# DeltaNet's values and outputs turned by VectorE and placed by the write to DRAM

## The chip, the cores and the metric

The kernel runs on one core of a Trainium2 chip. The metric is the device time of one execution in microseconds (us). Before the change it is 1200.37 us, the median of three runs (1199.62 to 1200.76).

## What is computed

One layer of a hybrid decoder over 1024 tokens of width 1024, in float32. One input projection feeds two mixers: a gated DeltaNet (4 heads of 128, computed in chunks) and a dilated sliding-window attention (8 heads of 64). Their outputs are concatenated, projected and added to the input; a gated MLP with a depthwise convolution follows, and a last norm. The change touches the DeltaNet mixer's values and outputs. The reference, cut to them:

```python
def gated_delta_rule(q, k, v, g, beta):
    ...
    rhs = jnp.concatenate([vc, gam * kc], axis=-1)
    sol = lax.linalg.triangular_solve(lmat, rhs, left_side=True, lower=True, unit_diagonal=True)
    u_v, w_k = sol[..., :Dv], sol[..., Dv:]
    ...
    def step(state, xs):
        uv, wk, qd, at, ke, ge = xs
        u = uv - jnp.einsum('bhck,bhkv->bhcv', wk, state)
        o = jnp.einsum('bhck,bhkv->bhcv', qd, state) + jnp.einsum('bhcj,bhjv->bhcv', at, u)
        state = ge[..., None, None] * state + jnp.einsum('bhck,bhcv->bhkv', ke, u)
        return state, o
    ...

def hybrid_layer(x, ...):
    h = rmsnorm(x, norm1_w)
    proj = h @ w_in
    ...
    qkv_a = jax.nn.silu(causal_dwconv(qkv_a, conv_qkv_w)).astype(jnp.float32)
    ...
    o_a = gated_delta_rule(qa, ka, va, g, beta)
    z = z_a.astype(jnp.float32).reshape(B, S, GDN_HEADS, GDN_HEAD_DIM)
    o_a = (rmsnorm(o_a, gdn_norm_w) * jax.nn.silu(z)).reshape(B, S, GDN_WIDTH).astype(x.dtype)
    ...
    x = x + jnp.concatenate([o_a, o_b], axis=-1) @ w_out
```

## The kernel before

**Layouts.** The projection leaves each of its columns (128 features) as a tile of 128 features by 1024 tokens, features on partitions. The DeltaNet chain wants values with tokens on partitions: a tile `vtok` of 128 tokens by 8 chunks by 128 features. Its outputs come out in that layout too, and the output projection wants features on partitions again. So values and outputs must be turned, 128x128 by 128x128, 8 such blocks a head each.

**Order on TensorE.** The `Weave` class plans one fixed order of TensorE's instructions. Each piece of work is a generator with a level; a generator yields how long it wants to wait by the planner's own costs, and the planner takes the ready one of the lowest level. A `slack` is added to a wait, so it says how long after an operand's planned time the consumer is placed. The projection (`dense`) is the filler of the highest level: 25 columns in the order of the list `DENSE` (line 42), each 48 matmuls of 128x512 (two halves, 8 rows of k, three products of high and low parts), written by `mm3`. The other engines' orders come from the scheduler, which follows what the tiles wait for; operations through `uv` and `ua` are given high priority. Nearly all DMAs are issued by SyncE (SP), in order. Because the operations run through helpers, most rows of the profile carry a helper's line: L139 and L141 for other engines and DMAs, L192 for matmuls, L196 for 128x128 transposes.

**The work around the change**, in the order in which the chip meets it:

- `dense` (507) evicts each half column from PSUM with VectorE into `xr` (or `aqkv` for attention's columns). For a query, key or value column `conv_silu` adds the causal convolution (three VectorE steps) and the silu (ScalarE), giving `qT`, `kT` or `vT`.
- `kprep` (586) and `qprep` (640) transpose keys and queries on TensorE for their norms, and make the chunk matrices; `qprep` parks query and matrix in DRAM (`qpark`, `atpark`).
- `vprep` (666) calls `tokens` (567): two batches of four TensorE transposes of `vT` into PSUM, then eight ScalarE activations that scale by the key's norm `nk` on the way into `vtok`.
- `forward_sub` (672) inverts the 32x32 blocks of all heads on VectorE (31 steps on `xi`) and stores `xi` and its turned copy `mt` to `xdram` and `xtdram`. `merges` (700) loads them (`x`, `um`) and builds the 128x128 inverses on TensorE; its first products are the group `x,um`.
- `chain` (798) runs the 8 chunks of one head, four heads interleaved, each step in turn on TensorE, VectorE and ScalarE. Its result goes back into `vtok`.
- `finish` (867) transposes a head's outputs on TensorE (two batches of four), ScalarE copies each PSUM bank to `ot` times the norm weight `gw2`, and SP stores it to `mixer`.
- The last four projection columns are the gates (`z`). Each loads its head's outputs (`og` from `mixer`); `gate` (483) multiplies them by silu of the column, and `mixer_splits` (1081) splits the gated head into high and low parts `ohi` and `olo` for `out_proj`.
- `attention` (902) waits for the chains of heads 0 and 1, then for the outputs of all heads (`("o", h)`), then for its first columns, and loads its operands with `att_load` (884). Each of its four groups takes a pair of heads.

Of the kernel before, what the change touches and what calls it, by code (L numbers as in the profile page):

```python
# [38 lines left out]
TSLACK = -1.0, -0.6  # L39
URGENT = 400  # L40
MGAP = 0.6
DENSE = ([("k", 3), ("a", 0, 0), ("a", 0, 1)] + [(c, h) for h in range(4) for c in "qv"] + [("a", 0, 2)]
         + [("a", p, i) for p in (1, 2, 3) for i in range(3)] + [("z", h) for h in range(4)])

# [100 lines left out]
def hybrid_layer(tc, I, out):  # L145
# [25 lines left out]
    def A(name, tag, dt=F32, shape=(P, 1024)):  # L171
        if tag in TURNS:
            i = turns[tag] = turns.get(tag, -1) + 1
            tag = TURNS[tag][i % len(TURNS[tag])]
        return tile_(lp, shape, dt, name, tag, SLOTS[tag])
# [72 lines left out]
    apark = dp.tile([4, 2, P, S], F32, name="apark")  # L248
    avdram = dp.tile([4, 32, 32, P], F32, name="avdram")
    qpark = dp.tile([H, P, S], F32, name="qpark")  # L250
    atpark = dp.tile([H, P, S], F32, name="atpark")
    xpark = dp.tile([KT, P, S], F32, name="xpark")
    upark = dp.tile([FT, P, S], F32, name="upark")
# [4 lines left out]
    def next_bank(tag, *tiles, slack=0.0):  # L258

        while max(wv.need(*tiles), wv.slot_free(tag, 2)) + slack > 1e-3:  # L260
            yield max(wv.need(*tiles), wv.slot_free(tag, 2)) + slack
        return bank(tag)

    def half(i):
        return slice(i * 512, i * 512 + 512)
# [180 lines left out]
    def scaled(pair, name, by_class=False, tag="ev", t=None, hs=(0, 1)):  # L446
        if t is None:
            t = A(name, tag)
        for h in hs:
            sl = half(h)  # L450
            if by_class:
                ve.tensor_tensor(t[:, sl].rearrange("p (n c u) -> p n u c", n=4, c=4),
                                        pair[h].rearrange("p (n u c) -> p n u c", n=4, c=4),
                                        rstdB[:, sl].rearrange("p (n u c) -> p n u c", n=4, c=4), op=OP.mult)
            else:
                ve.tensor_tensor(t[:, sl], pair[h], rstdB[:, sl], op=OP.mult)
        return t
# [22 lines left out]

    put_off = []

    def gate(og, xr, anchor=None):
        y = A("zz", "ev")
        insts = [ac.activation(y, xr, AF.Tanh, scale=0.5),
                 ve.scalar_tensor_tensor(y, y, 1.0, xr, op0=OP.add, op1=OP.mult),
                 ve.tensor_tensor(og, og, y, op=OP.mult)]
        last["og"] = insts[2:]
        if anchor is not None:
            after(insts[0], anchor[0], "the softmax goes first")  # L490
            after(insts[1], anchor[1], "the softmax goes first")
# [15 lines left out]
    def dense():  # L507

        yield from wv.until("first")
        yield from wv.until("norms")  # L510
        wv.add(2, first_keys())

        raw = [raw_weight(I["wi"][0])]
        nxt = wk(None, raw.pop())
        raw.append(raw_weight(I["wi"][1]))
        for i, col in enumerate(DENSE):
            kind, h = col[:2]
            if kind == "z":
                yield from wv.until(("o", h))
            w = nxt  # L520
            if i + 1 < len(DENSE):
                nxt = wk(None, raw.pop())
            if i + 2 < len(DENSE):
                raw.append(raw_weight(I["wi"][i + 2]))
            pair = []
            for hh in range(2):
                pt = bank("hf")
                yield wv.need(pt, *w)
                for k in range(KT):
                    mm3(pt, [t[:, k, :] for t in w], [t[:, half(hh)] for t in xs[k]], k == 0, k == KT - 1)  # L530
                    yield 0.0

                pair.append(pt)
                if hh == 0:
                    while put_off:
                        gate(*put_off.pop(0))
                    xr = A("aqkv" if kind == "a" else "xr", "go" if kind == "k" else "ev")
                scaled(pair, "xr", kind == "a", t=xr, hs=(hh,))
            if kind == "k":
                T["k", h] = conv_silu(xr, 4 + h, "kT", "kT*")  # L540
                wv.add(3, kprep(h))
            elif kind == "q":
                q = conv_silu(xr, h, "qT", "qa")
                wv.add(4, qprep(h, q))
            elif kind == "v":
                v = conv_silu(xr, 8 + h, "vT", "qa")
                wv.add(4, vprep(h, v))
            elif kind == "z":
                og = gated[h] = A("og", "kT*")
                sy.dma_start(og, mixer[h])  # L550
                if i + 1 < len(DENSE):
                    put_off.append((og, xr))
                else:
                    gate(og, xr)
            else:
                if col[2] < 2:
                    sy.dma_start(apark[h, col[2]], xr)
                else:
                    t = A("avt", "ev")
                    ve.transpose(t.rearrange("p (c n j) -> p n c j", c=4, n=NCH), by_block(xr))  # L560
                    for b in range(4):
                        sq_.dma_start(avdram[h].rearrange("u x (b j) -> b u x j", b=4)[b],
                                     t[32 * b:32 * b + 32].rearrange("u (x j) -> u x j", j=32))
                wv.done.add(col)
        wv.done.add("dense")

    def tokens(src, dst, scale=None, ss=None):

        for hh in range(2):
            pt = yield from next_bank("atr", src)  # L570
            for c in range(4):
                i = 4 * hh + c
                tp(pt[:, c * P:(c + 1) * P], src[:, i * P:(i + 1) * P])
            if dst is not None and scale is None:
                ua.activation(dst[:, half(hh)], pt, AF.Copy)
            for c in range(4):
                i = 4 * hh + c
                if scale is not None:
                    ua.activation(dst[:, i * P:(i + 1) * P], pt[:, c * P:(c + 1) * P], AF.Copy,
                                         scale=scale[:, i:i + 1])  # L580
                if ss is not None:
                    sq = tile_(sp, [P, P], F32, "sq", ("osq", "w2", "w3")[i % 3], 1)
                    ua.activation(sq, pt[:, c * P:(c + 1) * P], AF.Square, accum_out=ss[:, i:i + 1])
        return dst
# [80 lines left out]

    def vprep(h, vT):
        yield from wv.until(("q", h))
        yield wv.need(vT, slack=SLACK)
        G[h]["vtok"] = yield from tokens(vT, A("vtok", ("dv", "dw")[h % 2]), G[h]["nk"])
        wv.done.add(("v", h))  # L670

    def forward_sub():
# [192 lines left out]
        wv.add(1, finish(h, vtok))  # L865

    def finish(h, osb):
        for hh in range(2):
            pt = yield from next_bank("atr", osb, slack=0.8)
            for c in range(4):  # L870
                i = 4 * hh + c
                tp(pt[:, c * P:(c + 1) * P], osb[:, i * P:(i + 1) * P])
            ot = tile_(sp, [P, 512], F32, "ot", "t2", 2)
            ac.activation(ot, pt, AF.Copy, scale=gw2)
            sy.dma_start(mixer[h][:, half(hh)], ot)
        wv.done.add(("o", h))


# [23 lines left out]
    def attention():  # L902
# [1 line left out]
            yield from wv.until(("c", h, NCH - 1))  # L904
        mk = A("mk", "go", shape=(P, 448))
        sy.dma_start(mk, I["mk"])
        for h in range(H):
            yield from wv.until(("o", h))
        yield from wv.until(("a", 0, 2))
        cur = att_load(0)  # L910

        def scores(pair):

# [167 lines left out]
    def mixer_splits():  # L1081
        yield from wv.until("dense")
        load_residual(MORDER[0])
        load_residual(MORDER[1])
        wv.done.add("residual")
        for i in range(8):
            yield from wv.until(("o", i))
            ots[i] = (X("ohi"), X("olo"))
            if i < H:
                lo = split(gated[i], *ots[i])  # L1090
                last.setdefault("olo", []).append(lo)
                if i and "probabilities" in last:
                    after(lo, last["probabilities"], "the probabilities go first")
            else:
                src = A("ot", "ev")
                for h in range(2):
                    sl = half(h)
                    if i < 7 or h == 0:
                        sy.dma_start(src[:, sl], mixer[i][:, sl])
                    split(src[:, sl] if i < 7 or h == 0 else last["oT"], *[t[:, sl] for t in ots[i]])  # L1100
            yield wv.need(*ots[i])
            wv.done.add(("ot", i))
# [656 lines left out]
```

## Time and profile before

| | us |
|---|---|
| median of three runs | 1200.37 |
| the profiled execution | 1200.24 |
| its span | 1198.5 |
| stage from the projection's key columns to the merges' loads | 97 to 184 |
| merges | 184 to 225 |
| chain | 225 to 292 |
| from the chain's end to attention's first scores | 292 to 311 |
| attention, with the rest of the projection | 311 to 470 |

The page gives busy time per engine over the whole span. A row of a group reads: line, engine, operation, outputs and inputs by the program's names, shape, count, then busy us and mean ns of one, then the engine's idle time just before. A row of the timeline reads: start, busy time, engine, line, operation, names, shape and count of what runs in a row; a bracket at its end is the idle time before it and what ended that. Starts are in us from the span's start.

### The profile page before, as it was taken

What the parts mean: (1) busy time and instruction counts of PE and PEld (TensorE: products, weight loads), DVE (VectorE), ACT (ScalarE), POOL (GpSimd) and SP (SyncE); (2) the same over time, 40 slices, a digit from 0 to 9 for tenths busy, and PEclk for the clock granted to TensorE, in tenths of its full rate; (3) what the DMA queues carried; (4) which work ended last, traced back from release to release, by engine and by line L of the source; (5) the groups of instructions that cost most, each with busy time, mean ns of one, the idle gap of its engine ahead of it and who ended that gap; (6) DMA issues with size and microseconds to landing.
All of it is one profiled execution on the core that took longest, in us unless ns stands there. A gap on an engine that the chain in (4) does not pass through costs nothing.

```text
span 1198.5 us, 18275 instructions
## 1 busy us (share of the span) xinstructions
PE 1187.8 (99%) x7026; PEld 983.1 (82%) x7026; DVE 962.0 (80%) x1536; ACT 571.4 (48%) x1121; POOL 55.1 (5%) x50
## 2 busy tenths in 40 slices
PE   9999999999999999999999999999999999999997
PEld 7888888898777777888888888888888888888887
DVE  7686985584677687777898888989888889898987
ACT  7383344363444344555454544445454453445452
POOL 0212110013000000000000000000000000000001
PEclk9999999999999999999999999999999999999999
DMA  7323234537543314343222223131222395356734
GB/s 237 106 75 103 75 121 131 150 114 216 163 118 104 98 37 146 144 158 106 74 71 102 85 74 106 53 106 58 101 89 70 104 378 212 118 182 218 238 100 156
DMA packets 97448, 152.72 MB, mean 127 GB/s; under 512 B 37808, under 2 KB 48848, under 8 KB 97360
## 3 DMA queue, kind: packets, MB, share of 16 engines
q1 hardware_dynamic: 96640, 151.02, 38.5%
q8 instruction: 55, 0.90, 0.3%
q10 hardware_dynamic: 720, 0.53, 0.1%
q14 instruction: 33, 0.27, 0.1%
HBM read 115.59 MB, written 35.93 MB: 126 GB/s over the span
## 4 chain that ended last, share of the span: by engine, by line
PE 96%; DVE 2%; ACT 1%; issue 1%; DMA 0%; POOL 0%; DVEq 0%; ACTq 0%; POOLq 0%
PE ps L192 46%; PE pa L192 20%; PE dw L192 17%; PE pc L192 10%; PE ps L196 1%; PE ps L201 1%; DMA wst<-in_wu 0%; DVE sm L141 0%; PE warm L192 0%; DVE x1h L139 0%; ACT sm L141 0%; DVE aqkv L139 0%; DVE T L139 0%; DVE wst L139 0%; DVE pair L139 0%
## 5 line engine op out<-in xcount | busy, mean ns | idle before, releaser
L192 PE MATMUL dw<-pr 128*128 128x512 f32 (+1 forms) x984 | 211.4, 376 | 0.0
L192 PEld LDWEIGHTS dw<-pr 128*128 128x128 f32 x984 | 176.7, 188 | 33.7
L192 PE MATMUL ps<-xhi,whi 128*128 128x512 f32 x448 | 184.5, 412 | 0.0
L192 PE MATMUL ps<-xhi,wlo 128*128 128x512 f32 x448 | 175.2, 391 | 0.0
L192 PE MATMUL ps<-xlo,whi 128*128 128x512 f32 x448 | 174.8, 390 | 0.0
L192 PE MATMUL pa<-T,pair 128*128 128x512 f32 x528 | 127.1, 390 | 0.3 <-ACT u L139 0.2
L192 PEld LDWEIGHTS pa<-T,pair 128*128 128x128 f32 x528 | 98.9, 188 | 21.3 <-ACT u L139 0.8
L192 PEld LDWEIGHTS ps<-xhi,whi 128*128 128x128 f32 x448 | 84.4, 188 | 19.5 <-issue 3.6
L192 PEld LDWEIGHTS ps<-xhi,wlo 128*128 128x128 f32 x448 | 84.1, 188 | 18.5
L192 PEld LDWEIGHTS ps<-xlo,whi 128*128 128x128 f32 x448 | 84.5, 189 | 14.3
L139 ACT ACTIVATE u<-pa 128x512 f32<-128x512 f32 x44 | 26.3, 599 | 109.7 <-PE pa L192 109.6
L139 DVE SCALAR_TENSOR_TENSOR y<-xu,fcw,y 128x1023 f32<-128x1023 f32 (+1 forms) x44 | 56.3, 1280 | 24.4 <-ACT y L139 24.4
L139 ACT ACTIVATE pr<-wd 128x1024 fp32r<-128x1024 f32 x33 | 35.0, 1061 | 76.1 <-DVE wd L139 36.9
L139 ACT ACTIVATE whi<-wst 128x1024 fp32r<-128x1024 f32 (+2 forms) x38 | 38.5, 1013 | 62.9 <-PE ps L192 52.7
L192 PE MATMUL pa<-B,A 128*128 128x512 f32 x264 | 63.5, 389 | 0.0
L192 PE MATMUL pa<-T,S 128*128 128x512 f32 x264 | 63.4, 389 | 0.0
L192 PE MATMUL pc<-B,pair 128*128 128x512 f32 x264 | 63.4, 389 | 0.0
L192 PE MATMUL pc<-T,S 128*128 128x512 f32 x264 | 63.4, 389 | 0.0
L139 DVE TENSOR_TENSOR wst<-wst 128x512 f32<-128x512 f32 x88 | 60.3, 686 | 0.8
L192 PE MATMUL ps<-B,pair 128*128 128x512 f32 x252 | 60.5, 389 | 0.0
L141 ACT ACTIVATE sm<-sm,mx 128x128 f32<-128x128 f32 (+7 forms) x64 | 35.5, 556 | 50.1 <-DVE mx L141 50.1
L192 PEld LDWEIGHTS pc<-B,pair 128*128 128x128 f32 x264 | 49.5, 188 | 10.3
(244 smaller groups left out, 2241.4 us busy)
## 6 DMA issues: line engine op xcount, KB each, us to landing
wst<-in_wu SPq DMA_DIRECT2D x44, 512.0 KB, 3.7
wd<-in_wd SPq DMA_DIRECT2D x44, 512.0 KB, 4.4
wst<-in_wi SPq DMA_DIRECT2D x25, 512.0 KB, 3.7
upark<-y SPq DMA_DIRECT2D x22, 512.0 KB, 3.6
r<-upark SPq DMA_DIRECT2D x22, 512.0 KB, 9.5
wa<-in_wd SPq DMA_DIRECT2D x22, 256.0 KB, 3.0
apark<-aqkv SPq DMA_DIRECT2D x8, 512.0 KB, 2.7
wst<-in_wo SPq DMA_DIRECT2D x8, 512.0 KB, 3.7
```

The costliest lines, as they stand in the source:

```text
L139: return getattr(eng, op)(*a, **kw)
L141: return getattr(eng, op)(*a, **kw)
L192: tc.stamp_issue_order_token(nc.tensor.matmul(dst, lhs, rhs, start=start, stop=stop, **kw).ins, TOKEN)
L196: tc.stamp_issue_order_token(nc.tensor.transpose(dst, src, ident).ins, TOKEN)
L201: tc.stamp_issue_order_token(nc.tensor.transpose(dst, src[rows], ident[rows, rows]).ins, TOKEN)
```

## The change

Values: `vprep` turns `vT` in place with one VectorE transpose, which turns each 32x32 block by itself; four stores to a new DRAM tile `vdram` put the blocks where they belong, one load brings back `vtok`, and eight activations scale it in SBUF. Outputs: `finish` turns 32x32 blocks with four VectorE transposes of 128x256 (tile `ft`, with a pause of 0.4 us of planned time after each) and stores once; the blocks are left in a permuted order in `mixer`. The gate columns are therefore written permuted on eviction, `og` is loaded by four DMAs with runs of 1 KB, and the gated heads are put back in token order by the split. The factor `gw2` moves into `gate`. Attention no longer waits for the outputs of all heads; it loads first and then waits for the chains of heads 2 and 3.

In number: 64 TensorE transposes and 8 `ot` copies go; 4 VectorE transposes of 128x1024 and 16 of 128x256 come, and SP issues 16 stores to `vdram`, 4 loads of `vtok`, 12 more loads of `og` and 4 fewer stores to `mixer`.

In the built order of TensorE, the projection matmuls ahead of the first merge product are as many as before; one `qT,kT` group of four has moved behind it, and each transposing batch of a query is 6 projection matmuls later. Between the last chain product and attention's first scores stand 6 projection matmuls (before: 72 and 8 transposes); 18 more stand inside the chain, and a block of 78 (before: 3 and 36) ahead of attention's third group. On VectorE the inversion's last steps and the copy of `mt` have moved behind the eviction of the last query's second half. On SP each load of `vtok` stands behind its four stores and waits for them.

```diff
+FSLACK = 0.5
...
+    vdram = dp.tile([H, P, S], F32, name="vdram")
...
+    def by_row(t):
+        return t.rearrange("p (a c i) -> p a c i", a=4, c=NCH)
+
+    def by_token(t):
+        return t.rearrange("p (c a i) -> p a c i", a=4, i=32)
+
     def gate(og, xr, anchor=None):
         y = A("zz", "ev")
         insts = [ac.activation(y, xr, AF.Tanh, scale=0.5),
                  ve.scalar_tensor_tensor(y, y, 1.0, xr, op0=OP.add, op1=OP.mult),
-                 ve.tensor_tensor(og, og, y, op=OP.mult)]
+                 ve.scalar_tensor_tensor(og, og, gw2, y, op0=OP.mult, op1=OP.mult)]
...
-                scaled(pair, "xr", kind == "a", t=xr, hs=(hh,))
+                if kind == "z":
+                    ve.tensor_tensor(by_row(xr)[:, :, 4 * hh:4 * hh + 4], by_token(pt), by_token(rstdB[:, half(hh)]), op=OP.mult)
+                else:
+                    scaled(pair, "xr", kind == "a", t=xr, hs=(hh,))
...
                 og = gated[h] = A("og", "kT*")
-                sy.dma_start(og, mixer[h])
+                for b in range(4):
+                    sq_.dma_start(og[32 * b:32 * b + 32].rearrange("j (a y) -> j a y", a=4),
+                                 mixer[h].rearrange("(a j) (b y) -> b j a y", a=4, b=4)[b])
...
     def vprep(h, vT):
         yield from wv.until(("q", h))
-        yield wv.need(vT, slack=SLACK)
-        G[h]["vtok"] = yield from tokens(vT, A("vtok", ("dv", "dw")[h % 2]), G[h]["nk"])
+        yield wv.need(vT, slack=1.0)
+        vtok, nk = A("vtok", ("dv", "dw")[h % 2]), G[h]["nk"]
+        ve.transpose(vT, vT)
+        blocks = vdram[h].rearrange("(a t) (c b i) -> b t c a i", a=4, c=NCH, b=4)
+        for b in range(4):
+            sq_.dma_start(blocks[b], vT[32 * b:32 * b + 32].rearrange("t (c a i) -> t c a i", c=NCH, a=4))
+        sy.dma_start(vtok, vdram[h])
+        yield wv.need(vtok)
+        for c in range(NCH):
+            cs = slice(c * P, (c + 1) * P)
+            ua.activation(vtok[:, cs], vtok[:, cs], AF.Copy, scale=nk[:, c:c + 1])
+        G[h]["vtok"] = vtok
         wv.done.add(("v", h))
...
     def finish(h, osb):
-        for hh in range(2):
-            pt = yield from next_bank("atr", osb, slack=0.8)
-            for c in range(4):
-                i = 4 * hh + c
-                tp(pt[:, c * P:(c + 1) * P], osb[:, i * P:(i + 1) * P])
-            ot = tile_(sp, [P, 512], F32, "ot", "t2", 2)
-            ac.activation(ot, pt, AF.Copy, scale=gw2)
-            sy.dma_start(mixer[h][:, half(hh)], ot)
+        yield wv.need(osb, slack=FSLACK)
+        t = A("ft", "kT*")
+        by_feature, src = t.rearrange("p (b c i) -> p b c i", b=4, c=NCH), osb.rearrange("p (c b j) -> p b c j", c=NCH, b=4)
+        for b in range(4):
+            ve.transpose(by_feature[:, b], src[:, b])
+            yield 0.4
+        sy.dma_start(mixer[h], t)
         wv.done.add(("o", h))
...
-        for h in range(H):
-            yield from wv.until(("o", h))
         yield from wv.until(("a", 0, 2))
         cur = att_load(0)
+        for h in range(2, H):
+            yield from wv.until(("c", h, NCH - 1))
...
-                lo = split(gated[i], *ots[i])
+                g4, hi4, lo4 = by_row(gated[i]), by_token(ots[i][0]), by_token(ots[i][1])
+                ac.activation(hi4, g4, AF.Copy)
+                lo = ve.tensor_tensor(lo4, g4, hi4.bitcast(F32), op=OP.subtract)
```

## The prediction

> **What bounds the kernel now.** I read the page's head and the engine shares of the chain that ended last.
>
> ```profile
> span 1198.5 us, 18275 instructions
> PE 1187.8 (99%) x7026; PEld 983.1 (82%) x7026; DVE 962.0 (80%) x1536; ACT 571.4 (48%) x1121; POOL 55.1 (5%) x50
> PE 96%; DVE 2%; ACT 1%; issue 1%; DMA 0%; POOL 0%; DVEq 0%; ACTq 0%; POOLq 0%
> ```
>
> TensorE (PE) is busy 99% of the span and carries 96% of the chain, so a matmul that is taken away is worth its time unless it stood in a wait. The view by windows shows that for the stages the change touches: projection with the first preparation, merges, chain, the stage between, attention. Columns are the window, its length, then each engine's busy us with its instructions, granted clock, DMA share, GB/s.
>
> ```profile
> core 0: us, PE busy (x) PEld busy (x) DVE busy (x) ACT busy (x) POOL busy (x), PEclk, DMA share, GB/s
> 97.00:184.00 87.00, 87.00 (x449) 73.91 (x448) 73.31 (x153) 34.84 (x94) 13.59 (x8) 1.00 0.31 99
> 184.00:225.00 41.00, 41.00 (x590) 35.28 (x589) 20.47 (x31) 14.84 (x41) 2.96 (x3) 1.00 0.55 153
> 225.00:292.00 67.00, 65.94 (x447) 59.86 (x446) 43.44 (x125) 37.26 (x137) 13.13 (x10) 1.00 0.45 149
> 292.00:311.00 19.00, 19.00 (x102) 15.11 (x101) 7.85 (x22) 5.52 (x14) 3.54 (x2) 1.00 0.79 198
> 311.00:470.00 159.00, 158.27 (x1699) 121.17 (x1698) 119.77 (x320) 66.69 (x201) 3.65 (x8) 1.00 0.32 99
> ```
>
> PE shows idle time of 1.06 us in the chain and 0.73 in attention, none elsewhere; the clock is full throughout. VectorE is the second engine: 84% busy in the first window, 65% in the chain.
>
> **What goes from PE.** 64 transposes, in two groups of the view by instruction.
>
> ```profile
> L196 PE MATMUL ps<-ident,vtok 128*128 128x128 f32 x32 | 4.6, 273 | 0.0
> L196 PE MATMUL ps<-ident,vT 128*128 128x128 f32 x32 | 4.2, 274 | 0.0
> ```
>
> The 273 ns of one overlap with the next, so I price a batch by the starts around it in the timeline (start, busy, engine, group).
>
> ```profile
> 127.36 0.40 PE L192 MATMUL ps<-xhi,wlo 128*128 128x512 f32 x1
> 127.60 1.04 PE L196 MATMUL ps<-ident,vT 128*128 128x128 f32 x8
> 128.39 0.47 PE L192 MATMUL ps<-xhi,whi 128*128 128x512 f32 x1
> 128.70 0.39 PE L192 MATMUL ps<-xlo,whi 128*128 128x512 f32 x1
> 128.93 0.40 PE L192 MATMUL ps<-xhi,wlo 128*128 128x512 f32 x1
> ...
> 271.37 0.60 PE L196 MATMUL ps<-ident,vtok 128*128 128x128 f32 x4
> 271.73 0.48 PE L192 MATMUL ps<-xhi,whi 128*128 128x512 f32 x1
> 272.05 0.39 PE L192 MATMUL ps<-xlo,whi 128*128 128x512 f32 x1
> ```
>
> Projection matmuls follow each other at about 0.227 us. Without the batch two of them, in the place of 128.39 and 128.70, would start at 127.60 and 127.83; the second came at 128.70, so eight transposes cost 0.88 us (0.09 of it the first matmul after them, 0.31 to its follower instead of 0.23). The group of four costs 272.05 − 271.37 − 0.227 = 0.45. The vT transposes stand as four eights: 3.5 us. Of the vtok ones six fours (2.7) and one eight (0.9): 3.6. **Sum −7.1.** The projection, the merges and attention keep their matmuls.
>
> **The value's new way.** Per head VectorE turns vT, SP issues four stores to DRAM (runs of 128 bytes) and one load that waits for them, and ScalarE scales eight tiles, now from SBUF.
>
> ```profile
> L139 DVE STREAM_TRANSPOSE avt<-aqkv 128x1024 f32<-128x1024 f32 x4 | 5.0, 1245 | 0.1
> L139 SPq DMA_DIRECT2D avdram<-avt x16: 584/664/2220, 212.8 to 397.8; - x16
> DMA to landing us min/median/max: 2.7/3.5/4.3
> qT<-apark SPq DMA_DIRECT2D x4, 512.0 KB, 3.8
> 179.68 2.16 ACT L141 ACTIVATE vtok<-ps,nk 128x128 f32<-128x128 f32 x8
> 183.92 1.06 ACT L139 ACTIVATE qT<-qT 128x1024 f32<-128x1024 f32 x1 [2.08 <-DVE qT L139]
> 189.51 1.03 PE L196 MATMUL ps<-ident,qT 128*128 128x128 f32 x8
> 225.82 0.94 PE L192 MATMUL ps<-vtok,um 128*128 128x128 f32 x7
> ```
>
> The second and third rows are the existing turned values' store (issue ns and landing, min/median/max), the nearest to the new one; the fourth is a load of the same size. So 1.25 + 3×0.66 + 3.5 + 3.8 + 2.16 ≈ 12.7 us from silu to scaled. Its cover is the time until PE's first product with vtok at 225.82: head 3's stores stand in SP's queue behind the merge loads (issued until about 196, below), so its values are ready at about 210, 15 us early. If that cover were gone, the 12.7 would stand open once. The nearer danger is what queues behind: SP sits about 3.5 us in the load's wait for each head, and ScalarE's eight scalings stand ahead of the next head's query silu. For head 2 the scalings end near 184.8, the silu near 185.9; PE wants that query at 189.51, pulled ahead by three vT batches (2.64) and pushed back 1.36 by six projection matmuls that the built order puts ahead of it: 188.2, so 2.3 us of room. Heads 0 and 1 have about 1.5. I cost it at nothing; at the bad ends (landing 4.3, 0.8 over; issue and load 1.1 over) heads 0 and 1 lose 0.4 each.
>
> **The merges.** In VectorE's built order the inversion's last steps and the copy of mt have moved behind the eviction of the last query's second half, and its convolution stands between them.
>
> ```profile
> 174.02 0.32 SPq L139 DMA_DIRECT2D xdram<-xi  x1
> 175.15 0.32 SPq L139 DMA_DIRECT2D xtdram<-mt  x1
> 177.90 0.69 DVE L139 TENSOR_TENSOR xr<-ps,rstdB 128x512 f32<-128x512 f32 x1 [2.78 <-PE ps L192]
> 178.76 1.23 DVE L139 TENSOR_TENSOR wlo<-wst,whi 128x1024 fp32r<-128x1024 f32 x1 [0.17 <-ACT whi L139]
> 179.91 3.92 DVE L139 SCALAR_TENSOR_TENSOR qT<-xr,gcw,qT 128x1023 f32<-128x1023 f32 x3
> 178.36 1.91 SPq L139 DMA_DIRECT2D x<-xdram  x4
> L139 SPq DMA_DIRECT2D um<-xtdram x16: 432/449/487, 180.4 to 189.9; - x16
> DMA to landing us min/median/max: 1.8/1.9/3.6
> 198.42 2.21 PE L192 MATMUL ps<-x,um 32*32 32x32 f32 x128
> ```
>
> After: xr cannot start before 177.90 − 2×0.88 = 176.1; its 0.69, wlo's 1.23 and one of the three convolution steps (3.92 / 3 = 1.3) make 179.4, and the short end of the inversion puts its store at about 179.7 instead of 174.02. The load of x began 4.34 after the store, so 184.0; from it to the last um load's issue were 11.5 us, so 195.6, and its landing (median 1.9) 197.4. PE arrives at 198.42 − 3×0.88 − 0.9 (a qT,kT group, which the built order puts behind the merges) = 194.9; the last head's products come three quarters of 2.21 later, at 196.5. So the wait that is late next is um's loads, by 0.9 us: I take **+1.0**, ends 0 (a store two microseconds earlier) and 2.6 (landing 3.6).
>
> **Outputs and the chain.** Two batches and two ScalarE copies a head go; four VectorE transposes of 128x256 and one store come.
>
> ```profile
> L139 ACT ACTIVATE ot<-ps,gw 128x512 f32<-128x512 f32 x8 | 5.4, 685 | 8.2 <-PE ps L196 6.9 <-DMA mixer<-ot 1.2
> 238.76 1.05 DVE L139 TENSOR_TENSOR aqkv<-ps,rstdB 128x512 f32<-128x512 f32 x1 [0.24 <-PE ps L192]
> L139 DVE TENSOR_TENSOR xr<-ps,rstdB 128x512 f32<-128x512 f32 x32 | 22.0, 688 | 22.2 <-PE ps L192 22.2
> L139 DVE TENSOR_TENSOR aqkv<-ps,rstdB 128x512 f32<-128x512 f32 x24 | 26.3, 1096 | 26.1 <-PE ps L192 26.1
> ```
>
> A quarter of 1.245 is 0.31; xr and wlo give 0.69 for 512 and 1.23 for 1024, hence 0.42 for 256; I take 0.35, 5.6 us for sixteen. They raise VectorE's share of the chain window from 65 to 73%. A chain step that is ready may stand behind one: three heads by 0.42 at worst, 1.3; the eviction at 238.76, which stood before a chain step, may vanish (−1.05) or meet another (+1.05). Projection matmuls fill between chain steps, so I take **+0.5**, ends −1.0 and +2.4. The eight evictions of the gate columns are written permuted: between 688 and 1096 ns, at most 3.3 us of VectorE, and the four permuted splits by the same ratio 2.9; four loads replace one for each head's gate. All lie in the attention windows, where VectorE has 39 us free; if that cover were gone, they would cost those 6 us. The start of attention no longer waits for the outputs: 72 projection matmuls stood ahead of its first scores, now 6, while 18 more stand in the chain and a block of 78 behind attention's second group. They are moved, not removed; I take nothing.
>
> **Sum:** 1200.24 (the profiled execution: 1198.5 plus 1.74 around it) − 7.1 + 1.0 + 0.5 = 1194.6. That execution is 0.13 below the runs' median of 1200.37; on the median's scale I say **1194.8**.
>
> **Rivals.**
> - *No new wait* (1193.1). The sum with nothing for the merges and the chain. For it: PE's idle of 1.06 us shows how well the order covers; against: the inversion's store is built 5.7 us later.
> - *The waits eat it* (1199.0, no change). Every wait at its bad end: 1200.24 − 7.1 + 2.6 + 0.8 + 2.4. For it: 1.5 us of room for two queries is little and SP's queue runs in order; against: all bad ends must meet.
> - *The outputs' transposes were filler* (1198.2, no change). If the chain waits on its own latency, the 3.6 of the vtok groups gain nothing. For it: 0.36 us passes from each of those groups to projection work that is there anyway; against: only 1.06 us of idle in 67.
> - *VectorE takes over the path* (1203.7, slower). Its queue is in order. If each transpose stands ahead of an instruction that PE awaits, from the first vT on and then in the chain, 4×1.245 + 16×0.35 = 10.6 comes and 7.1 goes. It decides from the point where PE idles for VectorE at chain steps, for more than 7 us in all. For it: 84% in the first window; against: 35% free in the chain.
>
> The Trainium skill, "VectorE: DVE Perf Modes", section "🎯 Rules for kernel authors", gives a 128×128 transpose to TensorE where PSUM will do, since VectorE turns only 32×32 blocks (section "🔬 The three transpose paths"); by that rule the last rival would hold. The trace does not settle it: it shows both kinds of transpose here, and PE as the fuller engine.
>
> **How the numbers follow.** Forecast .45, no new wait .15, waits eat it .17, filler .10, VectorE .13. About 0.2% (2.4 us) is what a measurement can tell from no change: under 1198.0 is faster, over 1202.8 slower. Faster: .45 + .15 + .05 from the better ends of the two rivals at no change = .65; slower: .13 + .01 = .14; the same: .21. The range runs from the sum with all good ends (1200.24 − 7.1 − 1.0 = 1192.1) to 1201.0, past the waits' rival but short of the VectorE one, leaving out some .17. The forecast's own range is 1193.3 to 1196.6.
>
> **What would show it.** Right: no transposes of vT and vtok on PE; projection spacing at 0.227 where they stood; the first x,um product about 195 with a wait for um or x below 2.6 us ahead of its last quarter; vtok scaled more than 10 us ahead of vtok,um; every stage after the merges 5 to 7 us earlier. Wrong: PE waits for VectorE in the chain window beyond 2 us, a query transpose that waits for ScalarE, attention whose splits or gates come last, or the gates' loads on the chain of waits.

## The result, and the profile after

The changed kernel takes 1202.81 us (median of 12 runs, 1200.7 to 1207.1), the kernel before 1200.48 (12 runs, 1199.62 to 1202.31). The ratio is 1.0021, interval 1.0012 to 1.0030: **slower by 0.2%**, where 1194.8 was forecast. The profiled execution took 1202.19 with a span of 1200.4. Over the 12 runs the mean granted clock lay between 0.993 and 0.998, and the two runs at 0.993 are the two slowest, 1206.09 and 1207.1.

The page's head of the changed kernel, and the engine shares of its chain of waits:

```profile
span 1200.4 us, 18201 instructions
PE 1185.6 (99%) x6962; PEld 978.2 (81%) x6962; DVE 969.9 (81%) x1556; ACT 567.4 (47%) x1113; POOL 53.2 (4%) x50
PE 87%; DVE 4%; DMA 3%; issue 2%; ACT 1%; POOL 1%; SPq 1%; DVEq 0%; ACTq 0%; POOLq 0%
```

The 64 transposes are gone (7026 to 6962 matmuls), yet PE's share of the chain fell from 96 to 87%, and DMA and SP's queue stand in it now. The windows of the same stages:

```profile
97.00:184.00 87.00, 86.61 (x434) 73.12 (x434) 75.89 (x157) 33.10 (x86) 9.97 (x6) 1.00 0.45 119
184.00:225.00 41.00, 38.11 (x540) 32.19 (x539) 20.53 (x31) 16.86 (x48) 4.91 (x5) 0.96 0.74 186
225.00:292.00 67.00, 65.03 (x445) 57.27 (x444) 47.39 (x136) 32.76 (x127) 12.86 (x9) 1.00 0.44 144
292.00:311.00 19.00, 18.67 (x138) 14.07 (x137) 12.38 (x42) 7.82 (x24) 4.06 (x3) 1.00 0.88 194
311.00:470.00 159.00, 158.65 (x1661) 122.71 (x1660) 114.73 (x303) 64.28 (x193) 3.61 (x8) 1.00 0.37 105
```

In 184 to 225 PE idles 2.9 us (before: none), and for the first time the granted clock is not full there: 0.96. The timeline of that stage, picked rows in order:

```profile
173.35 1.24 DVE L140 STREAM_TRANSPOSE vT<-vT 128x1024 f32<-128x1024 f32 x1
174.62 1.29 SPq L140 DMA_DIRECT2D vdram<-vT  x2
176.70 2.31 SPq L140 DMA_DIRECT2D vdram<-vT  x2
180.54 0.19 DVE L140 TENSOR_TENSOR xi<-xi,tmp 128x31 f32<-128x31 f32 x1
182.46 0.33 SPq L140 DMA_DIRECT2D vtok<-vdram  x1
182.89 0.37 SPq L140 DMA_DIRECT2D xdram<-xi  x1
187.97 2.45 ACT L142 ACTIVATE vtok<-vtok,nk 128x128 f32<-128x128 f32 x8 [8.71 <-DMA vtok<-vdram]
190.31 1.91 SPq L140 DMA_DIRECT2D x<-xdram  x4
190.32 1.04 ACT L140 ACTIVATE qT<-qT 128x1024 f32<-128x1024 f32 x1
191.41 1.09 PE L197 MATMUL ps<-ident,qT 128*128 128x128 f32 x8 [2.02 <-ACT qT L140]
198.14 1.49 PE L193 MATMUL ps<-x,um 32*32 32x32 f32 x66
200.42 1.29 PE L193 MATMUL ps<-x,um 32*32 32x32 f32 x62 [0.79 <-DMA x<-xdram]
201.64 2.08 PE L193 MATMUL ps<-qT,kT 128*128 128x128 f32 x8
203.36 0.77 PE L193 MATMUL ps<-xhi,whi 128*128 128x512 f32 x1
```

It is read from the bottom up. The eight qT,kT products take 2.08 us and the projection matmul behind them 0.77 (before: 1.05, in the row below, and 0.48): PE runs at half speed there. Before that it waited 0.79 us for x, and ten us earlier 2.02 us for the last query's silu. The silu stood on ScalarE behind head 2's eight scalings, which waited 8.71 us for their load; the load stood on SP until its four stores had landed, and behind it the inversion's store (xdram), whose xi had been ready since 180.73. The same products in the kernel before:

```profile
196.07 1.05 PE L192 MATMUL ps<-qT,kT 128*128 128x128 f32 x8
```

The clock of the changed kernel in 2-us windows:

```profile
198.00:200.00 2.00, 1.55 (x67) 1.22 (x66) 1.49 (x6) 1.07 (x2) 0.89 (x1) 1.00 0.54 86
200.00:202.00 2.00, 1.58 (x63) 1.52 (x64) 1.97 (x3) 0.26 (x1) 0.00 (x0) 0.84 0.50 78
202.00:204.00 2.00, 2.00 (x10) 1.90 (x10) 0.95 (x3) 0.33 (x1) 0.00 (x0) 0.50 0.46 74
204.00:206.00 2.00, 2.00 (x9) 1.62 (x8) 0.88 (x4) 0.00 (x0) 0.00 (x0) 0.81 0.80 270
```

2 × (0.16 + 0.50 + 0.19) = 1.7 us are lost to the clock, with PE busy.

**A ledger.** Every kernel here has the same 1344 projection matmuls in the same sequence. For each, its start in one trace less its start in the trace of before, set to zero at number 430 (just ahead of the first vT batch), says how much has been gained (negative) or lost by there. Number 670 is the last of these points ahead of head 3's query transposes, 700 lies behind the first merge products, 730 behind the last vT batch, 820 in the chain ahead of the outputs, 1150 late in attention, where the orders agree again. Each line is one execution, and not always a middle one: those profiled took 1202.19 us for the changed kernel (median 1202.81), 1201.01 for v_only (1202.61), 1200.98 for late_t (1203.54) and 1197.98 for v_cured (1196.87).

| kernel | 670 | 700 | 730 | 820 | 1150 | ratio of times, interval |
|---|---|---|---|---|---|---|
| changed | −2.15 | +2.52 | +2.07 | +2.10 | +1.49 | 1.0021 (1.0012 to 1.0030) |
| v_only | −2.33 | +1.66 | +0.83 | +0.86 | +0.85 | 1.0016 (1.0007 to 1.0025) |
| f_only | 0.00 | 0.00 | +0.14 | +0.16 | −0.26 | 0.9998 (0.9989 to 1.0007) |
| pool_q | −2.02 | +3.54 | +2.74 | +2.78 | +2.19 | 1.0019 (1.0010 to 1.0028) |
| late_t | −1.99 | −2.01 | −2.83 | +1.94 | +1.33 | 1.0025 (1.0015 to 1.0035) |
| late_ld | −1.99 | −0.70 | −1.52 | +5.40 | +4.81 | 1.0043 (1.0028 to 1.0058) |
| f_late | 0.00 | 0.00 | 0.00 | +0.01 | −0.98 | 0.9997 (0.9988 to 1.0005) |
| hold_q3 | 0.00 | +5.71 | +5.73 | +5.75 | +5.78 | 1.0066 (1.0054 to 1.0078) |
| best1 | −2.75 | −2.72 | −3.46 | −1.98 | −3.52 | 0.9982 (0.9972 to 0.9993) |
| best2 | −2.75 | −2.72 | −2.58 | −2.55 | −4.15 | 0.9970 (0.9959 to 0.9982) |
| v_cured | −2.75 | −2.72 | −2.65 | −2.64 | −2.68 | 0.9969 (0.9960 to 0.9979) |
| att_early | 0.00 | 0.00 | 0.00 | −0.03 | +1.93 | 1.0018 (1.0009 to 1.0027) |

The chain's order differs a little between kernels, so the column 820 is good to some 0.5.

### The profile page after: what moved, and what is told of

The parts are those of the page before. It is cut to its first block, busy times and chain, and to the rows that moved or that the text cites. A ratio compares the mean times of both kernels' runs of the same rounds, so it can differ in the third digit from the quotient of the medians.

```text
span 1200.4 us, 18201 instructions
## 1 busy us (share of the span) xinstructions
PE 1185.6 (99%) x6962; PEld 978.2 (81%) x6962; DVE 969.9 (81%) x1556; ACT 567.4 (47%) x1113; POOL 53.2 (4%) x50
## 4 chain that ended last, share of the span: by engine, by line
PE 87%; DVE 4%; DMA 3%; issue 2%; ACT 1%; POOL 1%; SPq 1%; DVEq 0%; ACTq 0%; POOLq 0%
PE ps L193 37%; PE pa L193 20%; PE dw L193 17%; PE pc L193 10%; PE ps L202 1%; DMA vdram<-vT 1%; DVE vT L140 1%; SPq L140 1%; DMA vtok<-vdram 1%; POOL vtok L140 1%; PE ps L197 1%; DMA xdram<-xi 1%; DVE at L140 1%; ACT sm L142 0%; POOL ms L140 0%
## 5 line engine op out<-in xcount | busy, mean ns | idle before, releaser
L193 PEld LDWEIGHTS pc<-T,S 128*128 128x128 f32 x264 | 49.5, 188 | 10.3
```

Source lines behind the costliest of these rows:

```text
L193: tc.stamp_issue_order_token(nc.tensor.matmul(dst, lhs, rhs, start=start, stop=stop, **kw).ins, TOKEN)
```

## The experiments

### The two halves: v_only and f_only

v_only is the kernel before with the new vprep alone; f_only has all the rest of the change (new finish, permuted gates and splits, attention's waits) and the old vprep.

> Only the values are changed (their turn, four stores, load, eight scalings); outputs, gate columns and attention's waits are as before. Theory Q (the load that waits for its own stores holds up SP's queue, and the scalings behind it hold up ScalarE's): by the ledger of the changed kernel's trace, the first projection matmuls after the merges come 2.0 us late although 32 transposes (3.5 us) are gone, so this half alone loses: 1202 to 1203. Rival C (the values are fine, the outputs' half loses): this half gains 2.5 to 3.5: 1197 to 1198.

> Only the outputs are changed (turned by VectorE, permuted gate columns and splits, attention's waits); values go through TensorE as before. Theory Q: this half has nothing of the queues' loss; its 3.6 us of transposes are gained less what the chain waits more: 1197 to 1199.5. Rival C: this half loses, 1202 or more. If it gains the whole 3.6 (1196.9), the chain's extra waits in the changed kernel come from the values' half too.

v_only took 1202.61 us, f_only 1199.85, against 1200.68. The values' half makes the change slower, as theory Q had it. It waits for the last query's silu like the changed kernel, but here the clock falls to one half at once, and the products behind the wait take 1.92 us in place of 1.09 (a row of v_only's timeline):

```profile
191.43 1.92 PE L196 MATMUL ps<-ident,qT 128*128 128x128 f32 x8 [2.15 <-ACT qT L139]
```

The outputs' half gains nothing that can be told from none; its median lies just above the 1197 to 1199.5 expected. Its chain, in f_only's timeline:

```profile
269.75 1.90 POOL L140 TENSOR_TENSOR vtok<-vtok,ms 128x1024 f32<-128x1024 f32 x1
270.50 2.23 DVE L140 TENSOR_TENSOR wlo<-wst,whi 128x1024 fp32r<-128x1024 f32 x1
270.69 0.49 PE L193 MATMUL ps<-wke,ktok 128*128 128x128 f32 x2 [0.97 <-ACT w L142]
272.65 0.34 DVE L142 SCALAR_TENSOR_TENSOR ct<-ct,ge,ps 128x128 f32<-128x128 f32 x1
273.04 0.49 PE L193 MATMUL ps<-ct,kT 128*128 128x128 f32 x2 [1.19 <-DVE ct L142]
```

PE waits twice for a chain step, 0.97 and 1.19 us, in the midst of the turns of heads 0 and 1. The step ct came late because wlo took 2.23 us where it takes 1.2 elsewhere: it began while GpSimd's multiply ran (269.75 to 271.65) and ended 1.08 us after it. The last section comes back to this.

### The queue of the load: pool_q

```diff
-        sy.dma_start(vtok, vdram[h])
+        Engine(wv, nc.gpsimd, "sync", 0.05, 0.00142, 2.2).dma_start(vtok, vdram[h])
```

> The changed kernel with the four loads of vtok issued by GpSimd in place of SP; every other engine's order is the same. Theory Q: SP no longer waits for the stores, so the inversion's store leaves at about 181.2 in place of 182.9, the wait for x and the low clock behind it shrink or go, 1.5 to 2.5 us better than the changed kernel (1200.5 to 1201.3); the 2.0 us wait of a query transpose for ScalarE stays. Rival V (VectorE's order alone makes the inversion late): no better than 0.5 us, the store leaves as soon as the inversion ends either way.

It took 1203.37 us against 1200.68: no better. SP was freed, and the inversion's store left at 181.03; but the load came no sooner. Its row names mt as what ended GpSimd's idle time, yet the last of the four stores had landed only at 182.59, 0.6 us ahead of the load. It landed 6.4 us after its issue (5.5 in the changed kernel); ScalarE waited 10.41 us for it, and PE longer for ScalarE than in the changed kernel. The wait for x is gone, so rival V named the time but not the reason. Rows of pool_q's timeline:

```profile
183.19 0.59 POOL L140 DMA_DIRECT2D vtok<-vdram  x1 [11.67 <-DVE mt L140]
189.58 2.44 ACT L142 ACTIVATE vtok<-vtok,nk 128x128 f32<-128x128 f32 x8 [10.41 <-DMA vtok<-vdram]
193.02 1.09 PE L197 MATMUL ps<-ident,qT 128*128 128x128 f32 x8 [3.70 <-ACT qT L140]
```

So of the two queues behind the load, ScalarE's is the costly one here; SP's, on which I had put the 1.5 to 2.5 us, is not the first that ends late.

### Later turns, later loads: late_t and late_ld

```diff
+        turn = ve.transpose(vT, vT)
+        if "umload" in last:
+            after(turn, last["umload"])
```

late_t holds the turns of heads 2 and 3 (with all that follows) behind the last load of um; late_ld puts the same condition on the load of vtok instead.

> The changed kernel with the turns of heads 2 and 3 (and so their stores, loads and scalings) placed behind the last merge load; VectorE's end of the inversion then stands ahead of the last query's second eviction again. Theory Q and rival V both say that the wait for x, the low clock and the 2.0 us wait for the query's silu go: 4 to 5 us better than the changed kernel, 1198 to 1199, with vtok still in time for the chain. Rival C: at most 1 us better, since the loss is in the chain.

> The changed kernel with the loads of vtok of heads 2 and 3 (and so their scalings) behind the last merge load; the turns and stores stay where they are. Theory Q: SP lets the inversion's store go as soon as VectorE is done (181.0 in place of 182.9), ScalarE makes the last query's silu without waiting, so TensorE's 2.2 us wait there goes: 1198 to 1200. Rival V (VectorE's late inversion is what costs): TensorE then reaches the merges 2 us earlier and waits 2 to 3 us for x and um, with the low clock behind it: 1201.5 to 1203.

Both missed: 1203.54 us against 1200.68, and 1206.18 against 1200.31. The ledger says why: both cures work where they are put (late_t stands at −2.83 at number 730, all but some 0.7 of the values' 3.5), and both lose it again inside the merges. The scalings, now later, stand ahead of ScalarE's copies there. In late_ld PE also still waits 1.07 us for x at 197.86, though the silu is on time and SP lets the inversion's store go at 180.48: about so much the later inversion on VectorE costs by itself, less than the 2 to 3 us of rival V and with the clock at 1.00. late_ld's timeline:

```profile
218.27 2.44 ACT L142 ACTIVATE vtok<-vtok,nk 128x128 f32<-128x128 f32 x8 [5.98 <-DMA vtok<-vdram]
220.74 1.08 ACT L140 ACTIVATE x<-ps 64x512 f32<-64x512 f32 x2
221.39 2.82 PE L193 MATMUL ps<-um,x 64*64 64x64 f32 x24 [2.39 <-ACT x L140]
```

In late_t it was head 2's scalings and the copies of um: PE waited 1.46 us, and then ran at half speed for nearly 7 us (a row of late_t's timeline, then its windows):

```profile
211.89 4.37 PE L193 MATMUL ps<-x,um 64*64 64x64 f32 x48 [1.46 <-DVE um L140]
```

```profile
212.00:214.00 2.00, 2.00 (x29) 2.00 (x29) 1.94 (x3) 1.39 (x2) 0.00 (x0) 0.77 0.90 305
214.00:216.00 2.00, 2.00 (x22) 2.00 (x20) 1.97 (x3) 1.55 (x6) 0.00 (x0) 0.50 0.81 219
216.00:218.00 2.00, 2.00 (x7) 1.56 (x6) 1.01 (x2) 1.98 (x6) 0.00 (x0) 0.50 0.86 232
218.00:220.00 2.00, 2.00 (x6) 1.55 (x5) 0.00 (x0) 0.00 (x1) 0.00 (x0) 0.52 1.12 341
```

2 × (0.23 + 0.50 + 0.50 + 0.48) = 3.4 us for a wait of 1.5. In late_ld the window behind the wait is worse, 11 × 0.46 = 5.1 us, and another 1.7 us are lost to the clock at 572, behind the ledger's last point:

```profile
220.00:231.00 11.00, 9.61 (x70) 9.01 (x71) 1.36 (x2) 2.98 (x7) 0.00 (x0) 0.54 0.88 225
```

### The price of a wait: hold_q3

```diff
+            for _ in range(6 * (j == 3)):
+                nc.scalar.activation(y, y, AF.Copy)
             ac.activation(y, y, AF.Silu)
```

> The kernel before with six more copies of the last query onto itself on ScalarE ahead of its silu, so that TensorE waits about 2 to 3 us for that silu at 189 and nothing else changes. Theory K (such a wait brings the granted clock down to one half for some us): the time grows by the wait plus 1.5 to 3.5 us, 1204 to 1207, with a stretch of clock 0.5 within some 5 us of the wait, and runs spread over several us. Rival: the time grows by the wait alone, 1202.5 to 1203.5, with the clock at 1.00.

It took 1208.07 us against 1200.31, +7.8 (ratio 1.0066), for one wait of 3.85 (a row of its timeline, then windows):

```profile
194.02 1.71 PE L196 MATMUL ps<-ident,qT 128*128 128x128 f32 x8 [3.85 <-ACT qT L139]
```

```profile
194.00:196.00 2.00, 1.98 (x10) 1.89 (x11) 1.93 (x3) 1.02 (x9) 0.00 (x0) 0.58 1.01 387
196.00:198.00 2.00, 2.00 (x7) 1.56 (x6) 1.14 (x2) 2.00 (x11) 0.57 (x1) 0.56 0.89 303
...
572.00:577.00 5.00, 4.89 (x17) 3.89 (x17) 4.96 (x8) 3.00 (x5) 1.95 (x1) 0.66 0.00 0
```

The wait and the 2 × (0.42 + 0.44) = 1.7 us of low clock behind it make 5.6, and the ledger shows +5.71 there and no more up to number 1150. A second portion, 5 × 0.34 = 1.7 us, stands at 572 to 577, where the MLP begins and the kernel before keeps its full clock; why it comes there was not tried. Theory K is shown for the first portion: a wait of PE in this place costs more than itself. The time lies above its 1204 to 1207, since the wait was longer than the 2 to 3 us aimed at and the second portion was not expected. That the runs would spread was wrong, they lie within 1207.8 to 1209.1.

### The outputs after the chain, and attention's start: f_late and att_early

f_late is f_only with the turns behind the chain's last step, and attention waiting for all outputs again. att_early is the kernel before with the new waits of attention alone.

```diff
+        for i in range(H):
+            yield from wv.until(("c", i, NCH - 1))
...
+            after(ve.transpose(by_feature[:, b], src[:, b]), last["ms"])
```

> The outputs' half alone, with the turns of all heads held back until the last chain step and attention again waiting for all outputs. Theory D (VectorE's turns stand ahead of chain steps, and the early first scores wait for their softmax): both waits go, the 3.6 us of the transposes are gained: 1196.5 to 1197.8. Rival F (the transposes only filled time in which the chain waits anyway): no better than the outputs' half as it was, 1199.5 to 1200.5.

> The kernel before with nothing changed but attention's waits: it loads first and waits for the chains, not the outputs, so its first scores come 60 to 70 projection matmuls earlier. Theory D says that the early scores wait for their softmax: 0.5 to 1.5 us slower than before. The prediction's step (only moved, nothing): 1200.0 to 1200.8.

f_late took 1199.66 us against 1200.31, within the rival's bounds. But its ledger stands at −3.37 behind the chain (number 910), so the turns did stand ahead of chain steps, as theory D has it; then 2.4 of it are given back in attention. There PE waits longer for the softmax. First f_late's row of waits, then that of the kernel before:

```profile
PE ps L202 <- DVE sm L142: 1.8, 4, 0.6
```

```profile
PE ps L201 <- DVE sm L141: 0.4, 1, 0.4
```

That is 1.4 of the 2.4; the rest is open. att_early took 1202.31 us against 1200.34, more than expected: moving the first scores ahead of 60 projection matmuls (66 in the changed kernel), which I had costed at nothing, costs 1.9. Behind these scores stands a chain of ScalarE's table load, softmax steps and a normalisation on VectorE, and little is left on PE to cover it:

```profile
292.10 1.28 ACT L141 ACT_TABLE_LOAD   x1
294.08 1.90 POOL L139 TENSOR_TENSOR vtok<-vtok,ms 128x1024 f32<-128x1024 f32 x1
294.51 1.75 DVE L141 TENSOR_SCALAR sm<-sm,mx 128x128 f32<-128x128 f32 x2
296.11 0.47 PE L201 MATMUL ps<-ident,sm 64*128 64x64 f32 x4 [0.60 <-DVE sm L141]
```

The first of the two normalising steps took 1.55 us, where others of its shape take 0.27 to 0.29: it too began while GpSimd's multiply ran, and ended 0.08 us after it. In this stretch PE waits 0.60, 0.19 and 0.50 us, where the kernel before waits 0.36 once; so waits are 0.9 of the 1.9, and the rest is open.

### The cures together: best1, best2, v_cured

best1: head 2's turn behind the copy of mt; the loads of heads 2 and 3 behind the last load of um; the scalings of heads 0 and 1 behind the next query's silu, those of heads 2 and 3 behind ScalarE's copies of the first merge; f_late's outputs. best2 puts head 3's scalings behind the copies of the second merge products too. v_cured has best2's values and the outputs of the kernel before.

```diff
+        if "mt" in last and h >= 2:
+            after(turn, last["mt"])
...
+            inst = ua.activation(vtok[:, cs], vtok[:, cs], AF.Copy, scale=nk[:, c:c + 1])
+            after(inst, last["silu", h + 1] if h < 2 else last[("y1", "w2")[h - 2]])
```

> The changed kernel with all the cures: head 2's turn behind the inversion's end on VectorE, loads of heads 2 and 3 behind the last merge load, scalings behind the next query's silu (heads 0 and 1) or behind the first merge's copies (2 and 3), outputs turned after the chain with attention waiting for them. Theory Q with D: all 64 transposes are gained less 0.5 to 1.5 us of waits: 1194 to 1195.5. If something else costs (DMA traffic of the extra loads, rival C), 1198 or more.

> The version with all the cures, and head 3's scalings also moved, behind ScalarE's copies of the merges' second products. Theory Q: TensorE's 1.5 us wait for those copies goes, 1194.5 to 1196.5. Rival (the time of the value's way only moves on to the next wait): no better than 1197.5.

> The values' half alone with the cures of its queues; outputs and attention's waits as in the kernel before. Theory Q: the values' 3.5 us are gained, less up to 1: 1196.8 to 1198. Rival (turning the values through DRAM costs as much as it saves in any order): 1200 or more.

best1 took 1197.6 us against 1200.31, best2 1197.07 and v_cured 1196.87 against 1200.34: all are 0.2 to 0.3% faster than the kernel before. best1 missed its 1194 to 1195.5: PE waits 1.38 us for a copy of x that stands behind scalings on ScalarE, with the clock at 1.00. The window 184 to 225 of v_cured, where the changed kernel lost most, has its full clock again:

```profile
184.00:225.00 41.00, 40.29 (x584) 34.58 (x583) 23.12 (x36) 18.03 (x50) 3.01 (x3) 1.00 0.75 181
```

v_cured lies in its 1196.8 to 1198. Its median is 3.5 us lower (by the interval 2.5 to 4.8), which is what the vT transposes were priced at, but its traced execution shows only three of the four batches: −2.72 at number 700 and −2.65 at 730. The fourth batch's gain goes against 0.71 us of idle PE at 204.44, ahead of products of um and w, which the profile puts to issue, that is to no wait that it shows; best2 has 0.78 at the same place. What it is stays open. So the way through DRAM costs little where no queue that PE awaits stands behind it, and the theory that it must lose in any order falls. best2 missed its 1194.5 to 1196.5: its ledger ends 0.8 us ahead of v_cured's at the last projection matmul, but by the medians turning the outputs on VectorE adds nothing measurable.

## Why the prediction was wrong

By the ledger, the forecast's sum and what came of it:

| projection matmuls | forecast | measured |
|---|---|---|
| up to 670 (three vT batches) | −2.6 | −2.15 |
| 670 to 730 (one batch, merges) | −0.9 + 1.0 = +0.1 | +4.2 |
| 730 to 1150 (vtok transposes, chain, attention) | −3.6 + 0.5 = −3.1 | −0.6 |
| sum | −5.6 | +1.5 |

Of the +4.2, waits of 2.02 and 0.79 and 1.7 of low clock, less the 0.9 of a batch, make 3.6; the other 0.6 are not assigned.

- **What goes from PE: right.** Three batches and no other wait would be −2.64; the changed kernel lacks 0.5 of that, of which 0.40 is a first short wait for a query's silu. v_cured gained 3.5 by its median, and three of the four vT batches in its trace.
- **The value's way: the step that failed**, "I cost it at nothing". From the turn's start at 173.35 to the last scaling at 190.42 head 2 took 17.1 us, not 12.7: SP needed 174.62 to 179.01 for the stores (atpark among them) where I had 3×0.66, and the load landed 5.5 us after its issue where I had 3.8. The end of the query's silu, which I had put at 185.9 with 2.3 us of room, came at 191.36. I had named the right queue, ScalarE's, but taken the issue and landing times from other transfers of the kernel before; while head 2's load was under way (182 to 188) the DMA engines were busy for 0.83 of the time, against 0.55 in the kernel before. That this made the landing slower is argued, not shown. The bad ends that I listed for heads 0 and 1 came, larger, for head 2. v_only, which has this step alone, loses by itself.
- **The merges: the mechanism was right, the size near by luck.** VectorE did finish xi behind the last query's eviction (180.73; forecast some 179.7). SP then held the store to 182.89; it took 6.3 us to land (3.2 in the kernel before), and the load of x began 7.4 us after it, not 4.34. PE's wait, forecast at 1.0 for um, was 0.79 for x, and so short only because PE was already 2.0 late. The first x,um products came at 198.14 where I had 194.9.
- **No term for the clock.** The low clock took 1.7 us here. The profile of before shows a clock of 1.00 in every window quoted, so it had no row for it. hold_q3 shows that a wait alone, of 3.85 us, put into the kernel before, brings it down.
- **The chain and attention: mis-sized.** I took +0.5 with a bad end of 2.4 and nothing for the moved scores; 3.0 of the 3.6 were eaten. att_early prices the moved scores at 1.9; PE's longer waits in the changed kernel's chain are some 0.7; the rest is open. That the transposes only filled the chain's own waits is wrong: with the turns behind the chain f_late stands at −3.37 there. What it then gives back it loses in attention.
- **The rivals.** The waits did eat it, as the second rival said, but it stopped at 1199.0, with no term for the clock. "VectorE takes over the path" had nearly the right time, 1203.7, for another reason: in the changed kernel's chain PE idles for VectorE by 0.7 us by the view of waits (us, times, longest), not by the 7 that I named:

```profile
PE ps L193 <- DVE ct L142: 0.7, 2, 0.5
```

- **What was to show it**: the transposes gone, yes; "a query transpose that waits for ScalarE" was on the list of what would show it wrong, and is the row at 191.41.

Where the Trainium skill, "VectorE: DVE Perf Modes", section "🎯 Rules for kernel authors", gives 128×128 transposes to TensorE, v_cured differs for the values: 3.5 us faster by the medians without them on TensorE. For the outputs the rule holds in so far as nothing is gained (best2 against v_cured).

## What to carry to other kernels

Work taken off a full engine and sent the long way round (another engine, stores, a load that waits for them, another engine) is not free because its consumer is far off: list what stands behind each of its waiting instructions on every in-order queue, and price issue and landing by rows of that stage. A wait of TensorE can cost more than itself through the clock (1.46 us and 3.4 behind it in late_t), and need not (1.38 in best1). An order that hides a chain of softmax steps behind filler is part of the kernel's time; moving the scores is not free either.

## What the runs showed of the hardware

- **The clock.** In the traces' clock records the granted clock falls, apart from the last microseconds of every kernel, to 0.50 for 3.41 us or two or three times that, so the time lost comes in portions of 1.7 us: one in the changed kernel (behind a wait of 0.79 us, with 2.02 ten us ahead of it), in v_only (2.15) and in pool_q (3.70), two in late_t (1.46), three in late_ld (2.39), one in hold_q3 (3.85), and one more at 572 in the last two. The length of the wait does not decide it alone: behind the changed kernel's 2.02 the clock stayed at 1.00 for ten us, behind v_only's 2.15 at the same place it fell at once; best1's 1.38, late_ld's 1.07 and f_only's 0.97 and 1.19 left it at 1.00. The Trainium skill, "TensorE: Matmul & The Clock Gate", section "🔬 Part 1: The HAM clock gate (the "warmup" mystery)", has a clock halved by an activity window of about 3.4 µs that runs free; the portions agree. Its section "HAM oscillation — how this bites in real kernels" warns of gaps above some 3.4 µs; here shorter ones did it, two of them among the merges' small products.
- **VectorE beside GpSimd.** The one that begins first runs at its own pace, and the other ends later. In f_only GpSimd's multiply began first and took its usual 1.90 us; wlo, begun 0.75 us behind it, took 2.23. att_early's softmax step is the same case. In the changed kernel wlo began first, took its usual 1.22, and the multiply took 2.86:

```profile
269.54 1.22 DVE L140 TENSOR_TENSOR wlo<-wst,whi 128x1024 fp32r<-128x1024 f32 x1
269.66 2.86 POOL L140 TENSOR_TENSOR vtok<-vtok,ms 128x1024 f32<-128x1024 f32 x1
```

The kernel before has the same order and 2.59 for the multiply. The Trainium skill, "SBUF — State Buffer", section "🔬 SBUF: two separate sides", says that the two engines share a pair of ports by an exclusive lock; these rows agree. So VectorE reaching wlo 1 us later (270.50 against 269.54) put 1 us more into a step that PE awaits.
